# The opening of a transformer layer written as one list: squares in pairs on TensorE, low parts on VectorE, four tiles in the first batch

## The chip, the cores and the metric

The kernel runs on one core of a Trainium2 chip. The core has five engines, each with its own queue of instructions that it works off in order: TensorE (PE in the profile, with its weight loads as PEld), VectorE (DVE), ScalarE (ACT), GpSimd (POOL) and SyncE (SP), which here issues transfers. PSUM, into which TensorE adds up, is used here as eight banks of 128 x 512 numbers.

The metric is the device time of one execution in microseconds (us). The kernel before takes 1415.44 us, the median of 3 runs (1415.26 to 1416.74). The profile comes from one execution of its own, which took 1416.67 us.

## What is computed

One layer on 1024 positions of width 1024, in float32. Cut to what the change touches:

```
cond = silu(c)                                  # one row of 1024
mod  = cond @ w_ada + b_ada                     # six vectors of 1024: shift and scale here, others later
h    = rms_norm(x, g) * (1 + scale) + shift     # the opening
proj = h @ w_in                                 # k, v, 4 tiles of q, 8 of the mLSTM's q and k, its v, its gates, its output gate
...                                             # attention with rotary angles; a bidirectional mLSTM; output projection; FFN; final norm
```

The root mean square is taken over the width of `x`, for each position.

## The kernel before

**Layout.** `x` lies transposed: eight slices of 128 rows (width) by 1024 columns (positions), each handled as two halves of 512 columns. A sum over the width is thus a sum over the partitions of all slices, and a matmul with a matrix of ones makes it and spreads it over all partitions.

**Precision.** A product is made of three fast matmuls: each factor is split into a high part (a copy rounded to the matmul's format, made by ACT) and a low part (the rest, by a subtraction). `mm3` (L297) does high times high (L298), weight high times input low (L299), weight low times input high (L300). Weight tiles come as pieces of 128 x 512: loaded to `wst`, split to `whi` by ACT and to `wlo` by POOL (L436 to L447). `ones` and the sums of squares are plain float32, and such a matmul is recorded as two instructions.

**The opening (L490 to L610).** The condition row is broadcast to 128 partitions by its transfer and put through Silu. Sixteen half slices are squared by ACT and added up by DVE and POOL into `ssx`; after warming matmuls (L550) two matmuls (L552) finish the sum, and `rstd_steps` (L533) makes the reciprocal root: ACT's root, one step of refinement on DVE. In between, `w_ada` arrives in blocks of 128 x 1024: block `j` times the condition, summed along the row (`ada_load`, L509), gives 128 numbers of `mod`; slice `k` needs blocks `k` (shift) and `8+k` (scale). Block 0 is summed by POOL and ACT, the others by one DVE instruction. Then for each slice (`h_steps`, L561): DVE multiplies by the root, ACT applies scale and shift, ACT makes the high part `hh`, POOL the low part `hl` (DVE for slice 0).

**The first batch (L600 to L610).** Three tiles of 128 output columns, the keys, the values and the first query tile, are summed up side by side over the eight slices: 3 tiles x 2 halves x 8 slices x 3 = 144 matmuls, in six banks, with two more for the sums of squares. Behind it come units one after the other (the list `IN`, L48): the gates with half of the values (`("t", 0)`, matmuls 272 columns wide), three query tiles of 48 matmuls each, then mLSTM tiles. The finished keys go through `rope_steps` (L616): two copies out of PSUM by ACT, a swap of rows by transfers, multiplications with the angles on POOL and DVE, a root, and at the end two copies `k2` split by ACT and POOL. A query tile goes through the same steps, without the copies. Attention starts when the last query tile and the gates' chain are done.

**What sets the order.** A planner in the kernel's Python code (`Clock`, L125) runs as the program is written. It keeps its own time, with a cost for each operation of DVE, ACT and POOL (`Engine.cost`, L99) and for transfers; `ck.chain` starts each step at the time at which it believes the last one to be over, `ck.pe` moves its time on for matmuls, and a unit goes on when its inputs are due. What it writes is a fixed order for each engine; the waits are real. `dve`, `act` and `gps` are the engines as the planner counts them; `nc.vector` and the like are the engines uncounted. `psum_any` takes a bank without telling the planner that it is in use.

## Time and profile before

| | |
|---|---|
| median of 3 runs | 1415.44 us (1415.26 to 1416.74) |
| profiled execution | 1416.67 us, span 1414.9 us |
| mean granted TensorE clock | 0.970 |
| first projection matmul | at 35.93 us |
| first matmul of the gate unit, behind the first batch | at 88.64 us |
| idle of TensorE from 160 to 208 us | 9.2 us (48.0 less 38.83 busy) |

A line of the timeline gives the start and the duration in us, the engine, the line of the program, the operation, the tile written and the tiles read, the shapes, how many such instructions follow one another, and in square brackets how long the engine stood idle before and what ended that. `L96` is the line of a helper through which most operations of DVE, ACT and POOL pass, so these are told apart by their tiles. TensorE's matmuls overlap in part, so their durations say less than the distance from one start to the next.

### The profile page before, as it was taken

Reading aid. Unit: us, or ns where it says so; the run is one execution under the profiler, and the core shown is the slowest. Engines: PE = TensorE matmul, PEld = TensorE weight load, DVE = VectorE, ACT = ScalarE, POOL = GpSimd, SP = SyncE. Lnnn points to the kernel's source line nnn. Section 1 sums busy time; section 2 is a strip of 40 time slices with the busy share of each in tenths; the row PEclk is TensorE's granted clock in tenths of the full one; section 3 lists DMA queues with packets and bytes.
Section 4 is the critical chain, followed back from the end, with each engine's and each line's share of the span. In section 5 each row is a group of like instructions: output and inputs, shape, how many; then the busy total and the mean of one; then the engine's idle time right before and its main releaser. Section 6 shows DMA issues by size and latency. Waiting matters only on the chain.

```text
span 1414.9 us, 19493 instructions
## 1 busy us (share of the span) xinstructions
PE 1305.6 (92%) x6594; PEld 1076.0 (76%) x6602; DVE 1078.5 (76%) x1564; ACT 660.8 (47%) x1192; POOL 733.9 (52%) x591
## 2 busy tenths in 40 slices
PE   5789799999999989899987899999999999979997
PEld 2578677888878978777765788888888887867886
DVE  7947989987888938777699786676666654998876
ACT  6444326677666655454565233233333333444462
POOL 5555454544345336677658554545445445545542
PEclk9899989999999999999998999999999999989999
DMA  7446452322122146653641342323322259823324
GB/s 294 155 127 201 148 157 79 120 64 65 49 64 59 36 158 189 226 179 122 200 149 58 99 157 92 109 98 112 112 94 85 83 164 315 302 82 100 94 64 153
DMA packets 103171, 184.39 MB, mean 130 GB/s; under 512 B 11296, under 2 KB 32672, under 8 KB 103072
## 3 DMA queue, kind: packets, MB, share of 16 engines
q1 hardware_dynamic: 89968, 161.06, 35.9%
q10 hardware_dynamic: 13104, 22.10, 4.2%
q8 instruction: 52, 0.85, 0.3%
q14 instruction: 47, 0.39, 0.1%
HBM read 136.19 MB, written 43.25 MB: 127 GB/s over the span
## 4 chain that ended last, share of the span: by engine, by line
PE 60%; DVE 21%; DMA 6%; issue 5%; ACT 4%; POOL 4%; SPq 1%; ACTq 0%; DVEq 0%; POOLq 0%
PE acc L299 15%; PE acc L298 15%; PE acc L300 15%; DVE x L96 4%; DVE ada L96 3%; PE av L1028 3%; DVE sst L96 2%; PE T L1009 2%; DVE PT L96 2%; PE S L977 2%; DVE y L96 1%; PE acct L298 1%; PE acct L300 1%; PE acct L299 1%; DMA qd<-q_d 1%
## 5 line engine op out<-in xcount | busy, mean ns | idle before, releaser
L96 POOL TENSOR_TENSOR wlo<-wst,whi 128x512 fp32r<-128x512 f32 (+2 forms) x208 | 297.5, 1436 | 261.2 <-ACT whi L96 249.8
L96 ACT ACTIVATE whi<-wst 128x512 fp32r<-128x512 f32 (+2 forms) x219 | 131.5, 605 | 121.2 <-PE acc L300 26.5
L96 POOL TENSOR_SCALAR P<-P,sst 128x1024 f32<-128x1024 f32 x64 | 88.8, 1391 | 141.1 <-DVE sst L96 98.0
L299 PE MATMUL acc<-x,whi 128*128 128x512 f32 x352 | 139.9, 398 | 1.1 <-DVE x L96 1.1
L96 POOL TENSOR_TENSOR wlo<-wr,whi 128x512 fp32r<-128x512 f32 x60 | 82.9, 1382 | 80.6 <-ACT whi L96 79.3
L298 PE MATMUL acc<-hh,whi 128*128 128x512 f32 x224 | 97.5, 435 | 14.1 <-ACT hh L96 11.8
L298 PE MATMUL acc<-whi,wch 128*128 128x512 f32 x244 | 97.1, 398 | 5.7 <-ACT wch L96 5.7
L96 ACT ACTIVATE P<-S,sst,colq 128x1024 f32<-128x1024 f32 x64 | 77.2, 1206 | 52.4 <-DVE sst L96 46.8
L299 PE MATMUL acc<-hl,whi 128*128 128x512 f32 x224 | 92.4, 413 | 8.2 <-POOL hl L96 4.5
L300 PE MATMUL acc<-whi,wcl 128*128 128x512 f32 x244 | 97.0, 398 | 2.9 <-DVE wcl L96 2.8
L299 PE MATMUL acc<-wlo,wch 128*128 128x512 f32 x244 | 97.1, 398 | 0.1
L96 DVE SCALAR_TENSOR_TENSOR ada<-ada,cond 128x512 f32<-128x512 f32 (+1 forms) x79 | 81.2, 1036 | 17.6 <-DMA ada<-in_w_ada_dram 12.1
L300 PE MATMUL acc<-hh,wlo 128*128 128x512 f32 x224 | 91.5, 408 | 0.0
L96 DVE TENSOR_TENSOR sg<-acc,sg 128x512 f32<-128x512 f32 x67 | 45.3, 686 | 60.4 <-PE acc L300 60.0
L96 ACT ACTIVATE PT<-T 128x512 fp32r<-128x512 f32 x128 | 71.4, 597 | 37.6 <-PE T L1009 36.8
L96 ACT ACTIVATE whi<-wr 128x512 fp32r<-128x512 f32 x60 | 37.8, 632 | 109.1 <-DVE wr L96 51.1
L96 DVE TENSOR_TENSOR PT<-T,PT 128x512 fp32r<-128x512 f32 x128 | 82.7, 681 | 7.3 <-ACT PT L96 7.1
L298 PE MATMUL acct<-whi,hh 128*128 128x256 f32 (+1 forms) x256 | 79.4, 310 | 2.5 <-ACT xp L96 1.1
L96 DVE TENSOR_TENSOR wcl<-wd,wch 128x512 fp32r<-128x512 f32 x50 | 50.9, 1031 | 38.6 <-ACT wch L96 38.3
L1009 PE MATMUL T<-con,P 128*128 128x128 f32 x512 | 70.3, 275 | 10.3 <-DVE PT L96 7.4
L299 PEld LDWEIGHTS acc<-x,whi 128*128 128x128 f32 x352 | 66.9, 190 | 16.8 <-DVE x L96 1.6
L96 POOL TENSOR_TENSOR wlo<-s,whi 128x512 fp32r<-128x512 f32 x44 | 59.5, 1353 | 38.0 <-ACT whi L96 32.1
...
## 6 DMA issues: line engine op xcount, KB each, us to landing
...
```

The source lines that it names most:

```text
L96: return fn(*args, **kw)
L298: nc.tensor.matmul(acc, w[0], x[0], start=first, stop=False)
L299: nc.tensor.matmul(acc, w[0], x[1], start=False, stop=False)
L300: nc.tensor.matmul(acc, w[1], x[0], start=False, stop=last)
L977: nc.tensor.matmul(sp[:, halves(n)], qs[:, j * P:(j + 1) * P], k2[g][m][:, halves(n)], start=m == 0, stop=m == 1)
L1009: nc.tensor.transpose(tp[:, k], Pt[q][:, (4 * b + k) * P:(4 * b + k + 1) * P], ident)
L1028: nc.tensor.matmul(av, va[:, k, h // 4], PT[it][m][:, k], start=(k, m) == (0, 0), stop=(k, m) == (NJ - 1, 1))
```

## The change

The opening is no longer planned. It is written out as one list for each engine, on the engines uncounted:

- The condition arrives as one row (a tile of zeros with the row in its first partition), gets its Silu there, and is spread by matmuls with `ones`, from which ACT copies it to all partitions.
- Whole slices are squared. DVE adds each odd slice's squares to the even one's, and TensorE sums the four pairs in PSUM, 8 matmuls, with a warming matmul behind each of the first three pairs. The warming matmuls go from 9 and 6 to 3 and 5.
- Both factors, root and scale, go on in one DVE instruction (`xr`); ACT adds the shift as it makes the high part; DVE makes all low parts (`h_lo_of`). All dot products are on DVE. POOL keeps the low parts of the weights.
- The batch has four tiles, with the second query tile: 192 matmuls, all eight banks. Its weights are loaded at the start, some of them into tiles that are used for keys and values later. The second query tile leaves `IN`, and its rope steps wait for both key copies.
- The constants come later, and the copies of the masks stand behind the batch. The planner's time is set to 24 us at the start of the batch and goes on by 0.23 for each matmul.

The diff, cut to its core (removed lines of the old opening are those shown above):

```
-WARM = 6
-WARM0 = 9
-POOLED = (0,)
+WARM = 5
+WARM0 = 3
+NT0 = 4
 NB = 3
 KB = 5
 AHEAD = 2
 NP = NF // 2
-IN = ([("t", 0), ("q", 1), ("q", 2), ("q", 3), ("f", 0), ("f", 4), ("f", 1), ("f", 5), ("t", 2), ("f", 2), ("f", 6),
+IN = ([("t", 0), ("q", 2), ("q", 3), ("f", 0), ("f", 4), ("f", 1), ("f", 5), ("t", 2), ("f", 2), ("f", 6),
...
-    both = const.tile([P, 2], F32, name="both")
+    both = const.tile([P, 3], F32, name="both")
...
-    nc.scalar.dma_start(con, cons)
-    nc.vector.tensor_copy(selr, C("sel"))
...
+        cond0 = PP["cond"] = bp.tile([P, D], F32, name="cond", bufs=1)
-        va = kvp.tile([P, NJ, 2, P], F32R, name="va")
-        k2 = [[kvp.tile([P, S], F32R, name=f"k2{i}{g}") for i in range(2)] for g in range(2)]
...
-        specs = conv_w(0) + conv_w(1) + conv_w(2)
+        specs = []
...
-        load_cond(bp)
...
-                        (gps if n and k < 6 else dve).tensor_add(ssx[n], ssx[n], sq)
...
+        ve, ac, gp = nc.vector, nc.scalar, nc.gpsimd
...
+        spare = [kvp.tile([P, S], F32, tag=f"k2{i}", name="spare") for i in range(3)]
+        crow = kvp.tile([P, S], F32, tag="k23", name="crow")
+        room = [t[:, halves(i)].rearrange("p (a b) -> p a b", a=4) for t in spare for i in range(2)]
+        x_t = [stp.tile([P, S], F32, tag="x", name=f"x{k}", bufs=KT) for k in range(KT)]
+        gp.memset(crow, 0.0)
+        nc.sync.dma_start(crow[0:1], c)
+        for k in range(KT):
+            nc.sync.dma_start(x_t[k], xT[k])
+        ada_t, wst_t = {}, {}
+        def ada_load(j):
+            ada_t[j] = bp.tile([P, D], F32, tag="big", name="ada")
+            nc.sync.dma_start(ada_t[j], w_ada[j])
+        def first_load(b, f):
+            i = 4 * b + f
+            wst_t[b, f] = (wp.tile([P, 4, P], F32, tag="wst", name="wst", bufs=3) if i < 3 else room[i - 3])
+            nc.sync.dma_start(wst_t[b, f], w_f[f][:, 4 * b:4 * b + 4])
+        for j in (8, 0):
+            ada_load(j)
+        for f in range(NT0):
+            first_load(0, f)
+        for j in (9, 1, 10):
+            ada_load(j)
+        nc.sync.dma_start(con, cons)
+        for f in range(NT0):
+            first_load(1, f)
+        W0 = {}
+        def first_hi(b, f):
+            if (b, f) in ((1, 2), (1, 3)):
+                i = 2 * (f - 2)
+                if not i:
+                    W0["more"] = kvp.tile([P, 4, 4, P], F32R, tag="va", name="more")
+                W0[b, f] = [W0["more"][:, i + j] for j in range(2)]
+            else:
+                W0[b, f] = [wp.tile([P, 4, P], F32R, tag="w" + t, name="w" + t) for t in ("hi", "lo")]
+            ac.activation(W0[b, f][0], wst_t[b, f], AF.Copy)
+        def first_lo(b, f, eng):
+            eng.tensor_sub(W0[b, f][1], wst_t[b, f], W0[b, f][0].bitcast(F32))
+        def dot(j):
+            ve.scalar_tensor_tensor(ada_t[j], ada_t[j], 1.0, cond0, op0=OP.mult, op1=OP.mult, accum_out=modacc[:, 0, j:j + 1])
+        sc1 = stp.tile([P, KT], F32, name="sc1")
+        b1 = stp.tile([P, KT], F32, name="b1")
+        ve.tensor_scalar(b1, V("b_ada", 8, KT), 1.0, None, op0=OP.add)
+        def shift(k):
+            ve.tensor_add(mod[:, k:k + 1], modacc[:, 0, k:k + 1], V("b_ada", k))
+        def gain(k):
+            ve.scalar_tensor_tensor(sc1[:, k:k + 1], modacc[:, 0, 8 + k:9 + k], b1[:, k:k + 1], V("norm_mix_g", k),
+                                    op0=OP.add, op1=OP.mult)
+        cb = [psum_any([P, HALF], "acc") for _ in range(NH)]
+        ac.activation(both[:, 2:3], eps, AF.Silu)
+        ac.activation(crow[0:1], crow[0:1], AF.Silu)
+        ac.activation(both[:, 2:3], eps, AF.Abs_reciprocal_sqrt)
+        for n in range(NH):
+            nc.tensor.matmul(cb[n], ones, crow[:, halves(n)], start=True, stop=True)
+        msp = [psum_any([P, HALF], "ms") for _ in range(NH)]
+        acc0 = [[psum_any([P, HALF], "acc") for _ in range(NH)] for _ in range(2)]
         for _ in range(WARM0):
...
+            nc.tensor.matmul(acc0[0][0], ones, crow[:, 0:HALF], start=True, stop=True)
+        ssx = stp.tile([P, S], F32, tag="ssx", name="ssx")
+        sqw = kvp.tile([P, 2, S], F32, tag="va", name="sqw")
+        sqs = [ssx, sqw[:, 0], sqw[:, 1]]
+        for k in range(KT):
+            if k == 2:
+                for n in range(NH):
+                    ac.activation(cond0[:, halves(n)], cb[n], AF.Copy)
+            t = sqs[2] if k % 2 else sqs[k // 2 % 2]
+            for cs in [slice(0, S)] if k < KT - 1 else [halves(n) for n in range(NH)]:
+                ac.activation(t[:, cs], x_t[k][:, cs], AF.Square)
+                if k % 2:
+                    a = sqs[k // 2 % 2]
+                    ve.tensor_add(a[:, cs], a[:, cs], t[:, cs])
+            if k % 2:
+                for n in range(NH):
+                    nc.tensor.matmul(msp[n], ones, a[:, halves(n)], start=k == 1, stop=k == KT - 1)
+                if k < KT - 1:
+                    nc.tensor.matmul(acc0[0][0], ones, crow[:, 0:HALF], start=True, stop=True)
+        rv, ry = ([small() for _ in range(NH)] for _ in range(2))
+        rstd = ry
+        def root_v(n):
+            ve.tensor_scalar(rv[n], msp[n], 1.0 / D, EPS, op0=OP.mult, op1=OP.add)
+        def root_y(n):
+            ac.activation(ry[n], msp[n], AF.Abs_reciprocal_sqrt, scale=1.0 / D, bias=eps)
+        def root_end(n):
+            ve.scalar_tensor_tensor(rv[n], rv[n], -0.5, msp[n], op0=OP.mult, op1=OP.mult)
+            ve.scalar_tensor_tensor(ry[n], rv[n], 1.5, ry[n], op0=OP.add, op1=OP.mult)
         for _ in range(WARM):
...
+            nc.tensor.matmul(acc0[0][0], ones, crow[:, 0:HALF], start=True, stop=True)
+        def xr(k, n):
+            x = x_t[k][:, halves(n)]
+            ve.scalar_tensor_tensor(x, x, sc1[:, k:k + 1], rstd[n], op0=OP.mult, op1=OP.mult)
+        def h_hi_of(k, n):
+            ac.activation(h_hi[k][:, halves(n)], x_t[k][:, halves(n)], AF.Identity, bias=mod[:, k:k + 1])
+        def h_lo_of(k, n):
+            ve.scalar_tensor_tensor(h_lo[k][:, halves(n)], x_t[k][:, halves(n)], mod[:, k:k + 1],
+                                    h_hi[k][:, halves(n)].bitcast(F32), op0=OP.add, op1=OP.subtract)
+        dot(8)
+        gain(0)
+        root_v(0)
+        root_y(0)
+        ac.activation(msp[0], ry[0], AF.Square)
+        first_hi(0, 0)
+        first_lo(0, 0, gp)
+        dot(0)
+        shift(0)
+        root_y(1)
+        root_end(0)
+        first_hi(0, 1)
+        first_lo(0, 1, gp)
+        xr(0, 0)
+        h_hi_of(0, 0)
+        root_v(1)
+        ac.activation(msp[1], ry[1], AF.Square)
+        first_hi(0, 2)
+        first_lo(0, 2, gp)
+        h_lo_of(0, 0)
+        first_hi(0, 3)
+        first_lo(0, 3, gp)
+        root_end(1)
+        xr(0, 1)
+        h_hi_of(0, 1)
+        h_lo_of(0, 1)
+        def prepare(k):
+            if k + 1 < KT:
+                if k > 1:
+                    ada_load(9 + k)
+                ada_load(k + 1)
+            dot(8 + k)
+            gain(k)
+            dot(k)
+            shift(k)
             for n in range(NH):
...
+                xr(k, n)
+                h_hi_of(k, n)
+            for n in range(NH):
+                h_lo_of(k, n)
+            if k < 5:
+                first_hi(1, k - 1)
+                first_lo(1, k - 1, gp)
+        def mm(k, f, n, i):
+            w, h = W0[k // 4, f], (h_hi[k][:, halves(n)], h_lo[k][:, halves(n)])
+            a, b = ((0, 0), (0, 1), (1, 0))[i]
+            nc.tensor.matmul(acc0[f][n], w[a][:, k % 4], h[b], start=(k, i) == (0, 0), stop=(k, i) == (KT - 1, 2))
+        acc0 += [[psum_any([P, HALF], "acc") for _ in range(NH)] for _ in range(2)]
+        ck.until(24.0)
         for k in range(KT):
...
+            if k + 1 < KT:
+                prepare(k + 1)
+            seq = [(f, n, i) for n in range(NH) for f in range(NT0) for i in range(3)]
+            if k == 0:
+                seq = [(f, n, i) for n in range(NH) for i in range(3) for f in range(NT0)]
+            elif k == KT - 1:
+                seq = [(f, n, i) for f in range(NT0) for n in range(NH) for i in range(3)]
+            for f, n, i in seq:
+                mm(k, f, n, i)
+                ck.pe(0.23)
+                if n == 1 and i == 2 and (k == 3 or k == 7 and f < 2):
+                    load_piece()
+        va = kvp.tile([P, NJ, 2, P], F32R, tag="va", name="va")
+        k2 = [[kvp.tile([P, S], F32R, tag=f"k2{2 * g + i}", name=f"k2{i}{g}") for i in range(2)] for g in range(2)]
+        ve.tensor_copy(selr, C("sel"))
+        ve.tensor_copy(identb, ident)
+        for i in range(2):
+            ve.tensor_copy(maskb[:, 0, i], C("maskf"))
+            ve.tensor_copy(maskb[:, 1, i], C("maskb"))
         att = {}
...
         dexp = mid.tile([64, 2 * MH, NJ], F32, name="dexp")
         un = Stream(units(IN))
+        rope_steps(4, [(a, Flag()) for a in acc0[0]])
         v_steps([(a, Flag()) for a in acc0[1]])
-        rope_steps(4, [(a, Flag()) for a in acc0[0]])
         ck.at(2.5, lambda: rope_steps(0, [(a, Flag()) for a in acc0[2]]))
+        ck.chain(0.0, *k2_ok, lambda: rope_steps(1, [(a, Flag()) for a in acc0[3]]))
         for i in range(2):
             rp.append(stp.tile([P, S], F32, tag="x", name="rps", bufs=KT))
             dma(rp[i], rope[i])
```

89 lines of the change are left out of this document (removed).

## The prediction

> **What bounds the kernel now.** I read the page first, then the busy time of each engine in stretches of the opening and behind it, then the chain of waits and the opening instruction by instruction. The page shows TensorE (PE) busy 92% of the span, so a change that leaves its work alone can gain only where PE stands still.
>
> ```profile
> span 1414.9 us, 19493 instructions
> PE 1305.6 (92%) x6594; PEld 1076.0 (76%) x6602; DVE 1078.5 (76%) x1564; ACT 660.8 (47%) x1192; POOL 733.9 (52%) x591
> ```
>
> The stretches (columns: stretch, its length, busy time of PE, weight loads, VectorE (DVE), ScalarE (ACT), GpSimd (POOL), granted PE clock, DMA share, GB/s):
>
> ```profile
> 28.70:40.40 11.70, 0.80 (x1) 0.29 (x1) 11.63 (x19) 7.11 (x11) 6.30 (x5) 0.73 0.83 294
> 40.40:88.64 48.24, 39.02 (x144) 28.98 (x144) 35.70 (x52) 20.62 (x32) 27.20 (x18) 0.89 0.42 137
> 88.64:120.00 31.36, 31.36 (x239) 29.91 (x237) 21.59 (x38) 11.97 (x24) 12.90 (x7) 1.00 0.52 139
> 120.00:160.00 40.00, 36.70 (x160) 29.55 (x158) 35.38 (x42) 17.32 (x24) 25.70 (x15) 0.91 0.56 175
> 160.00:208.00 48.00, 38.83 (x161) 30.93 (x162) 38.81 (x61) 13.38 (x20) 24.23 (x17) 0.89 0.57 175
> 208.00:508.00 300.00, 283.95 (x1877) 249.39 (x1876) 252.90 (x431) 196.94 (x343) 131.14 (x98) 1.00 0.22 66
> ```
>
> In the opening PE waits and DVE works: DVE is busy 11.63 of 11.70 us just before the projection. From 40.40 to 88.64 PE runs 144 matmuls. How long these need unhindered is in the timeline of PE:
>
> ```profile
> 35.93 0.80 PE L298 MATMUL acc<-hh,whi 128*128 128x512 f32 x1 [7.24 <-ACT hh L96]
> 40.45 0.80 PE L299 MATMUL acc<-hl,whi 128*128 128x512 f32 x1 [3.73 <-DVE hl L96]
> 41.04 0.63 PE L300 MATMUL acc<-hh,wlo 128*128 128x512 f32 x1
> 41.47 0.63 PE L298 MATMUL acc<-hh,whi 128*128 128x512 f32 x1
> ...
> 56.95 0.50 PE L299 MATMUL acc<-hl,whi 128*128 128x512 f32 x1 [1.39 <-POOL hl L96]
> ...
> 77.72 0.79 PE L298 MATMUL acc<-hh,whi 128*128 128x512 f32 x1 [4.55 <-ACT hh L96]
> ...
> 83.02 0.40 PE L298 MATMUL acc<-hh,whi 128*128 128x512 f32 x1
> ...
> 88.64 0.29 PE L298 MATMUL acct<-whi,hh 128*128 128x272 f32 x1
> 88.77 0.29 PE L299 MATMUL acct<-wlo,hh 128*128 128x272 f32 x1
> ```
>
> The 24 matmuls from 83.02 to 88.64 take 5.62 us, 0.234 each; at the lower clock they are 0.43 apart (41.04 to 41.47). So 144 need 33.7 us of 48.2, and 14.5 us are waits and low clock. The chain of waits names DVE for them: the dot products (ada) and the scaling of the input (x) hold 37% of the chain up to 92 us.
>
> ```profile
> by line: DVE ada L96 22.1%; DVE x L96 15.2%; DVE mod L96 8.5%; DMA x<-in_xT_dram 7.6%; POOL ssx L96 6.6%; issue 4.6%; PE acc L299 3.9%; DVE hl L96 3.6%; PE acc L300 3.5%; DVE ssx L96 3.4%; PE acc L298 3.2%; ACT sq L96 2.7%; DVE sc L96 2.5%;
> ```
>
> **The gain on offer.** The change puts the first query tile's 48 matmuls into the opening batch. Before, that tile came behind the opening: 48 x 0.234 = 11.2 us. The old opening and that tile thus end, as PE time, at 88.64 + 11.2 = 99.8 us. The new batch, 192 x 0.234 = 44.9 us, has to be set against this.
>
> **Step 1, to the sum of squares.** The condition row now comes first, behind a memset of 0.95 us on POOL that the sync queue waits for; then Silu of one row. TensorE spreads the row to all partitions (2 full-precision matmuls), runs 3 for warmth, 8 for the squares with 3 between: 16, each recorded as two halves.
>
> ```profile
> 5.27 1.06 ACT L96 ACTIVATE cond<-cond 128x1024 f32<-128x1024 f32 x1 [2.34 <-DMA cond<-in_c_dram]
> 7.61 10.95 PE L550 MATMUL acc<-con,ones 128*128 128x512 f32 x18 [7.61 <-DMA con<-in_cons_dram]
> 12.86 0.34 PEld L550 LDWEIGHTS acc<-con,ones 128*128 128x128 f32 x1 [0.52 <-issue]
> 13.68 0.19 PEld L550 LDWEIGHTS acc<-con,ones 128*128 128x128 f32 x1 [0.48 <-issue]
> 14.11 0.19 PEld L550 LDWEIGHTS acc<-con,ones 128*128 128x128 f32 x1 [0.24 <-issue]
> 19.66 1.12 PE L552 MATMUL ms<-ssx,ones 128*128 128x512 f32 x2 [1.10 <-DVE ssx L96]
> 81.43 0.95 POOL L96 MEMSET gI<- 128x1024 f32 x1
> ```
>
> A half takes 0.43 us (13.68 to 14.11) once the clock is up and about 0.85 in the first 6.1 us (7.61 to 13.68; 7 halves). The old broadcast of half a megabyte had landed by 5.27; the row is 4 KB but issued 0.7 us later, so I take 4.1, and PE starts at 5.2. It is PE that sets this step: square 4 reuses the buffer that the first pair's matmuls read. 5.2 + 6.1 + 25 x 0.43 = 22.0 for the second half of the columns, 21.1 for the first; before it was 19.66 + 1.12 = 20.8. So the squares on TensorE gain nothing here, and freeing POOL of its additions gains nothing either. Bounds 20 to 22.5, from a row 1 us earlier or 1.2 us later.
>
> The Trainium skill, "TensorE: Matmul & The Clock Gate", section "Part 1: The HAM clock gate", has the clock up after about 3.4 us of work; the row above shows 6.1. By that rule, an estimate, the low-clock phase would be 2.7 us shorter, the step 1.3 us and the sum as much; I keep the row.
>
> **Step 2, to the first projection matmul.** Durations:
>
> ```profile
> 20.82 0.69 ACT L96 ACTIVATE sq<-ms,both 128x512 f32<-128x512 f32 x1 [1.01 <-PE ms L552]
> 24.68 0.59 ACT L96 ACTIVATE ms<-sq 128x512 f32<-128x512 f32 x1
> 31.69 0.61 ACT L96 ACTIVATE hh<-x 128x512 fp32r<-128x512 f32 x1
> 29.73 0.68 DVE L96 TENSOR_TENSOR x<-x,sq 128x512 f32<-128x512 f32 x1
> 30.33 1.22 DVE L96 SCALAR_TENSOR_TENSOR ada<-ada,cond 128x1024 f32<-128x1024 f32 x1
> 31.48 0.08 DVE L96 DVE_READ_ACCUMULATOR ada<-ada,cond 128x1 f32 x1
> 45.10 0.68 DVE L96 TENSOR_TENSOR x<-x,sq 128x512 f32<-128x512 f32 x1
> 47.38 1.30 POOL L96 TENSOR_TENSOR hl<-x,hh 128x512 fp32r<-128x512 f32 x1 [3.62 <-ACT hh L96]
> 49.48 2.31 DVE L96 SCALAR_TENSOR_TENSOR ada<-ada,cond 128x1024 f32<-128x1024 f32 x1
> 57.09 0.69 DVE L96 TENSOR_TENSOR x<-x,sq 128x512 f32<-128x512 f32 x1
> 73.95 2.35 DVE L96 TENSOR_TENSOR x<-x,sq 128x512 f32<-128x512 f32 x2
> ```
>
> A half row on DVE occupies 0.60 us (29.73 to 30.33), a dot product 1.15 (30.33 to 31.48). But a dot product beside a POOL operation takes 2.31: it stands until POOL is done. From 45.10 to 57.09 two of the eight 128-row slices pass: own work 4 x 0.6 + 4 x 1.15 + 0.5 small = 7.5 of 12.0 us, with four POOL operations, so each costs DVE 1.1 us. New order: root 0.69 (to 21.8), root_v and the second dot product on DVE to 23.2, two root steps and the scaling, 3 x 0.6, with two weight splits of POOL in between, 2 x 1.1 to 1.25: 26.9; high part on ACT, 0.61 to 0.81: first matmul at 27.7, against 35.93 before. Bounds 25.4 (POOL costs nothing) and 29 (one more operation, step 1 late).
>
> The Trainium skill, "SBUF — State Buffer", section "Who interferes with whom", has GpSimd and a VectorE operation with two SBUF inputs take turns on one port, held for the whole instruction: 1.30 per POOL operation instead of 1.1. By that, an estimate, the opening's ten operations below would end it 2 us later.
>
> **Step 3, the batch.** Slice 0 waits for its four weight tiles one by one (ACT 0.61, POOL 1.30 each): its last matmul is near 36. DVE goes on from 26.9 with one root_v, four half rows and a scaling (3.7), two POOL operations (2.2) and 1.1 of waiting for ACT, to 33.9; with slice 1's dot products, scaling and high part (2.5 + 0.6 + 0.6) its first matmul is ready at 37.5. From then on each slice needs on DVE two dot products 2.3, two small ones 0.2, two scalings and the two low parts 2.4, together 4.9, and about 0.4 of waiting for ACT's high part: 5.3. PE needs 5.6. Low parts moved from POOL add 1.2 us a slice to DVE, but POOL's 1.1 twice a slice go. What stays on POOL are weight splits: four of the second weight half, one per slice 1 to 4, then the next unit's, about three against slice 6 and one against 7. Starts of slices by DVE: 37.5, then 4 x (5.1 + 1.1) = 62.3 for slice 5, + 5.1 + 3.3 = 70.7, + 6.2 = 76.9 for slice 7. Behind it PE waits 0.7 for the low part, 0.5 for the second column half, and runs 5.4: **83.5**. So the fourth tile is covered by PE's waits, and the batch gains 99.8 - 83.5 = 16.3. Bounds: POOL free of cost, 35.5 + 0.7 + 7 x 5.6 = 75.4 (gain 24.4); each POOL operation 1.3 and step 2 at its late end, 88 (gain 11.8). ACT has 2 x 0.81 + 0.61 = 2.2 us a slice and hides. Weight and ada transfers hide too: POOL frees the staging tiles by 32, and an ada tile is asked for two slices (12 us) ahead.
>
> **Step 4, behind the opening.** Four tiles hold all eight PSUM banks. The pair of the fourth is read only when both key copies are ready:
>
> ```profile
> 119.18 5.21 POOL L96 TENSOR_TENSOR k<-kdup,k 128x1024 fp32r<-128x1024 f32 x2 [10.35 <-ACT k L96]
> 93.75 1.35 DVE L96 TENSOR_SCALAR sq<-ms 128x512 f32<-128x512 f32 x2 [17.44 <-ACT sq L96]
> 100.55 0.68 DVE L96 SCALAR_TENSOR_TENSOR sq<-sq,ms 128x512 f32<-128x512 f32 x1
> 8.12 0.22 DVE L295 CAST maskb<-con 128x128 bf16<-128x128 f32 x1
> ```
>
> Before, that was at 124.4, 36 us behind the batch. So the gate and value unit starts with six banks, while the key's root (2), the value's transposes (2) and the query's sums (1) want some, and DVE empties the unit's own late. Price: 0 if ACT, idle there, empties tiles 0 to 2 in time, 9 if PE stands behind the unit's first column block (88.64 + 24 x 0.13 = 91.8) until the root has read its banks (100.55); I take 2.5, nearer the first, since tiles 0 and 1 finish 18 and 12 matmuls, 4.2 and 2.8 us, before the batch does. The query's rope steps now load DVE and POOL beside the gates' chain: DVE is at 84% between 120 and 208 (35.38 + 38.81 of 88), so between 0 and 5; I take 1.5. The six small copies of masks move behind the opening: at most 6 x 0.22 us on DVE, idle there for 17.44 us, so nothing; without that cover 1.3.
>
> **Sum.** 16.3 - 2.5 - 1.5 = 12.3. The profiled run took 1416.67 us (span 1414.9 and 1.8 around it): 1404.4. It lies 1.2 above the median of 1415.44, so on the median's footing **1403**. Bounds of the parts together: gains of 24.4 and of -2.2 (11.8 - 9 - 5).
>
> **Rivals.** (A) DVE, not PE, sets the pace behind the opening as well. For: 84% there, and its idle 17.44 us before 93.75 is all that shrinks. Then the moved matmuls return as PE idle, and only the earlier end counts: 88.6 - 83.5 = 5.1, 1410. Against: from 208 to 508 PE is busy 284 of 300, DVE 253. (B) POOL costs DVE nothing, because its splits fall into DVE's waits: gain 24.4 - 2.5, about 1394. Against: 2.31 for 1.22. (C) Slower: the new pauses hold PE's clock down. A matmul at the low clock costs 0.43 - 0.234 = 0.196 more; from 78 such of 192 on (15.1 us) the change is over 0.2% slower, and with 120 (23.5) it is 11.2 slower, 1427. For: after pauses of 3.7 and 4.55 us the next ones are 0.43 apart. Against: after 1.39 us (56.95) they were not, and my longest pause is about 2.2. (D) The change lands but the order that the planner writes behind it does not close up: PE idle from 120 to 208, 3.3 + 9.2 = 12.5 us, doubles, and 12.3 are gone: 1415.5, no change.
>
> **How the numbers follow.** Forecast 0.56, A 0.20, B 0.08, C 0.06, D 0.10. About 0.2%, 2.8 us, is what a measurement of this kernel can tell from no change. Faster: forecast, B and most of A (0.18), 0.82. Same: 0.06 of D and 0.02 of A, 0.08. Slower: C and the 0.04 of D in which more than the gain goes, 0.10. The range leaves out C and the worst of D above, and half of B below: 1393 to 1414.
>
> **What would show it.** Sums of squares no earlier than 20 us; first projection matmul near 28; the batch's 192 matmuls ending between 80 and 87 with DVE above 90% busy; dot products near 2.3 beside a weight split and 1.22 elsewhere; waits of PE in the gate unit for ACT or DVE under 5 us together; attention's first scores 8 to 20 us earlier than before. The prediction is wrong in its core if the batch ends after 92, if its matmuls are 0.43 apart for more than 15 us, or if the batch ends as said and the scores start no earlier.

## The result, and the profile after

The changed kernel takes 1433.82 us (median of 4 runs, 1433.20 to 1434.39); the kernel before has a median of 1416.09 (4 runs). The recorded ratio is 1.0106, with a 95% interval of 1.0087 to 1.0124. The ratio stands for 15 us and the medians are 17.7 us apart, so the change is slower by 15 to 18 us; forecast was a gain of 12. The profiled run took 1433.2 us.

The opening itself came out nearly as predicted. From TensorE's timeline of the changed kernel (start, duration, then what ended the idle time before):

```profile
4.39 3.78 PE L564 MATMUL acc<-crow,ones 128*128 128x512 f32 x4 [4.39 <-ACT crow L561]
...
19.02 1.88 PE L586 MATMUL ms<-sqw,ones 128*128 128x512 f32 x4
...
27.05 0.73 PE L667 MATMUL acc<-hh,whi 128*128 128x512 f32 x2 [1.86 <-ACT hh L611]
...
72.97 0.50 PE L667 MATMUL acc<-hh,whi 128*128 128x512 f32 x1 [2.39 <-ACT hh L611]
...
86.05 0.39 PE L667 MATMUL acc<-hh,more 128*128 128x512 f32 x1
86.28 0.29 PE L292 MATMUL acct<-whi,hh 128*128 128x272 f32 x1
```

The first projection matmul is at 27.05 (before 35.93), and all four tiles are summed up at 86.28, where the three tiles took until 88.64. Counting the fourth tile's 11.2 us, the opening is 99.8 - 86.28 = 13.5 us better. Between 27.05 and 86.28 VectorE is the busier engine, with 52.58 of 59.23 us (TensorE 50.35), and from the second to the seventh slice it sets the pace, with 6.7 us or more a slice (see step 3 below):

```profile
27.05:86.28 59.23, 50.35 (x192) 36.68 (x193) 52.58 (x81) 20.35 (x35) 19.23 (x13) 0.97 0.44 148
```

So the loss is behind the opening. I cut both runs at three events that both have, the first scores of attention, its last value matmul (`av`) and the first sum of squares of the second norm, and read busy time by stretch (stretch, length, PE, weight loads, DVE, ACT, POOL, granted PE clock, DMA share, GB/s). Before:

```profile
0.00:205.10 205.10, 162.17 (x721) 124.61 (x722) 159.03 (x234) 88.41 (x137) 108.01 (x70) 0.92 0.56 182
205.10:504.80 299.70, 284.58 (x1872) 249.68 (x1870) 254.90 (x428) 196.56 (x342) 133.95 (x101) 1.00 0.23 67
504.80:695.20 190.40, 174.85 (x992) 148.22 (x998) 131.68 (x285) 95.02 (x235) 125.03 (x159) 0.97 0.58 186
```

After:

```profile
0.00:198.70 198.70, 169.12 (x750) 128.31 (x751) 155.70 (x230) 76.18 (x117) 84.19 (x53) 0.95 0.55 180
198.70:511.00 312.30, 296.18 (x1971) 262.85 (x1969) 257.13 (x438) 198.56 (x350) 132.88 (x101) 0.99 0.25 74
511.00:710.60 199.60, 165.78 (x871) 137.23 (x877) 129.22 (x285) 89.68 (x225) 120.80 (x154) 0.91 0.53 170
```

The lengths differ by -6.4, +12.6 and +9.2 us; what comes behind the third event takes 719.7 us before (1414.9 - 695.2) and 720.8 after (1431.4 - 710.6). Together that is the whole difference of the spans, 16.5 us, and each of the first three parts can be read further.

**Ahead of attention, -6.4 instead of -13.5.** The last rows of the gate columns come to VectorE behind an adaLN dot product whose load is late (timeline of VectorE after):

```profile
117.61 2.11 DVE L96 SCALAR_TENSOR_TENSOR ada<-ada,cond 128x512 f32<-128x512 f32 x1 [5.19 <-DMA ada<-in_w_ada_dram]
...
119.65 0.16 DVE L96 COPY gI<-acct 128x16 f32<-128x16 f32 x1
```

The gates' chain starts from that copy, at 119.65. In the kernel before, the last of the eight copies was at 117.3 (count, shortest/median/longest ns, first to last start):

```profile
L96 DVE COPY gI<-acct x8: 159/163/175, 96.2 to 117.3; 128x16 f32<-128x16 f32 x8
```

**In attention, +12.6.** TensorE stood still 16.1 us (312.30 - 296.18), before 15.1. TensorE did 11.6 us more in the longer stage, with 432 column matmuls of the value and output-gate units (`acct`, 3 x 144), before 312 (3 x 104). These are fill work: units that the planner puts wherever attention leaves TensorE free. That the stage is longer because of them is how I first read this; the experiments do not bear it out (e1 and e17 below). One of the three forms, before and after:

```profile
L298 PE MATMUL acct<-whi,hh 128*128 128x256 f32 x104 | 32.4, 312 | 1.5 <-ACT xp L96 1.1 <-ACT vstg L96 0.5
```

```profile
L292 PE MATMUL acct<-whi,hh 128*128 128x256 f32 x144 | 43.5, 302 | 0.0
```

**Behind attention, +9.2.** There TensorE had 9.1 us less to do and stood still for 33.8 us (199.60 - 165.78), before 15.6 (190.40 - 174.85). Groups of TensorE's instructions in that stretch, before and then after (count, busy time and mean, then idle time in front and what ended it):

```profile
L298 PE MATMUL acct<-whi,hh 128*128 128x256 f32 x88 | 28.0, 318 | 0.9 <-DVE avt L96 0.9
L1795 PE MATMUL ni<-Cs,mq 128*128 128x260 f32 x64 | 21.0, 411 | 6.8 <-DVE num L96 6.7
```

```profile
L292 PE MATMUL acct<-whi,hh 128*128 128x256 f32 x48 | 14.4, 300 | 0.9 <-DVE avt L96 0.9
L1875 PE MATMUL ni<-Cs,mq 128*128 128x260 f32 x64 | 21.6, 421 | 19.0 <-DVE num L96 19.0
```

Of the column matmuls 3 x 48 = 144 were left there, before 3 x 88 = 264, and the mLSTM's own matmuls waited 19.0 us for VectorE's `num` instead of 6.7. One place stands out. The column units ended at 537.3 us, the first output unit (`yah`) began at 558.1; before, 581.9 and 582.5. All matmuls of the two kinds, before and then after:

```profile
L300 PE MATMUL acct<-whi,hl x256: 274/282/293, 88.9 to 581.9; 128*128 128x256 f32 x96, 128*128 128x272 f32 x32
L298 PE MATMUL acc<-yah,whi x128: 389/397/793, 582.5 to 715.1; 128*128 128x512 f32 x128
```

```profile
L294 PE MATMUL acct<-whi,hl x256: 274/283/292, 86.5 to 537.3; 128*128 128x256 f32 x96, 128*128 128x272 f32 x32
L292 PE MATMUL acc<-yah,whi x128: 391/397/994, 558.1 to 730.5; 128*128 128x512 f32 x128
```

The timelines of TensorE and of VectorE at the end of that gap:

```profile
556.39 1.21 PE L1875 MATMUL ni<-Cs,mq 128*128 128x260 f32 x2 [8.58 <-DVE num L96]
```

```profile
554.72 0.69 DVE L96 SCALAR_TENSOR_TENSOR ada<-ada,cond 128x512 f32<-128x512 f32 x1 [0.78 <-DMA ada<-in_w_ada_dram]
...
555.63 0.61 DVE L96 SCALAR_TENSOR_TENSOR num<-ni,cols,num 128x130 f32<-128x130 f32 x2
```

No output unit may start before the last 16 half loads of `w_ada` are in, for the memory they use is given to the output units. When the column units run out, the kernel's loop (`while not summed`) takes the remaining loads one after the other, and the `num` that TensorE waits for stands behind them on VectorE. A second stop comes near the end of the stretch: TensorE waits 4.55 us for ScalarE's `yah`, up to 678.96, and 2.87 us for GpSimd's `yal`, up to 682.63. By then these loads have long been in.

### The profile page after: what moved, and what is told of

Read it like the earlier page. It is cut to its first block, busy times and chain, and to the rows that moved or that the text cites. A ratio compares the mean times of both kernels' runs of the same rounds, so it can differ in the third digit from the quotient of the medians.

```text
span 1431.4 us, 19460 instructions
## 1 busy us (share of the span) xinstructions
PE 1314.7 (92%) x6602; PEld 1081.2 (76%) x6610; DVE 1074.5 (75%) x1569; ACT 645.8 (45%) x1171; POOL 706.5 (49%) x572
## 4 chain that ended last, share of the span: by engine, by line
PE 56%; DVE 25%; issue 6%; POOL 4%; DMA 4%; ACT 4%; SPq 0%; DVEq 0%; ACTq 0%; POOLq 0%
PE acc L293 14%; PE acc L294 14%; PE acc L292 14%; DVE sst L96 4%; DVE y L96 3%; DVE x L96 3%; PE av L1108 3%; DVE PT L96 2%; PE S L1057 2%; PE T L1089 2%; DVE ada L96 1%; DVE ada L545 1%; POOL wlo L96 1%; DVE qg L96 1%; POOL wv L96 1%
## 5 line engine op out<-in xcount | busy, mean ns | idle before, releaser
L96 POOL TENSOR_TENSOR wlo<-wst,whi 128x512 fp32r<-128x512 f32 (+2 forms) x200 | 288.2, 1447 | 267.2 <-ACT whi L96 257.1
L96 ACT ACTIVATE whi<-wst 128x512 fp32r<-128x512 f32 (+2 forms) x211 | 126.2, 605 | 118.9 <-PE acc L294 26.6
L96 POOL TENSOR_TENSOR wlo<-wr,whi 128x512 fp32r<-128x512 f32 x60 | 83.5, 1392 | 79.7 <-ACT whi L96 77.0
L96 DVE TENSOR_TENSOR PT<-T,PT 128x512 fp32r<-128x512 f32 x128 | 83.7, 682 | 12.7 <-ACT PT L96 12.5
L96 DVE TENSOR_REDUCE sst<-S 128x1 f32<-128x1024 f32 x64 | 77.7, 1214 | 4.8 <-PE S L1057 4.8
L96 DVE SCALAR_TENSOR_TENSOR x<-acc,mod,x 128x512 f32<-128x512 f32 (+1 forms) x92 | 62.6, 717 | 17.3 <-PE acc L294 17.1
L1108 PE MATMUL av<-PT,va 128*128 128x256 f32 x512 | 70.4, 283 | 4.0 <-DVE PT L96 4.0
L292 PE MATMUL acc<-hh,whi 128*128 128x512 f32 x160 | 70.3, 440 | 3.0 <-ACT xp L96 3.0
```

The lines of the kernel that those rows point to most:

```text
L96: return fn(*args, **kw)
L292: nc.tensor.matmul(acc, w[0], x[0], start=first, stop=False)
L1108: nc.tensor.matmul(av, va[:, k, h // 4], PT[it][m][:, k], start=(k, m) == (0, 0), stop=(k, m) == (NJ - 1, 1))
```

## The experiments

From the result I had two theories. *Lost cover*, or *stock*: the 48 matmuls moved into the first batch were fill work; the units behind them move up, and the stock is too small where the mLSTM's own chains set the time. *Order*, or *draw*: the planner writes a new order for any change ahead of it, and the kernel before happens to have a good one. A third, *gap*, came up on the way: the loop over the loads.

**e1_hold.** Lost cover taken back: the column units stop during attention with 264 matmuls left, as before (eleven chunks of 24; the "33" in the text below is a slip).

```
+ held = Flag()
...
- yield [pieces[w0 + k // 2][2]] + (...)
+ yield [pieces[w0 + k // 2][2]] + (...) + ([held] if (ci, j, k) == (1, 5, 0) else [])
...
  ck.streams([Stream(values()), Stream(turned()), Stream(scores())], [un])
+ held.set(ck, ck.t)
```

> The changed kernel, but its last 33 column chunks of the fill units t1 and t3 (264 matmuls of 256 columns, the number that the kernel before had left) are held back until the attention stage is over; nothing else is changed. Theory 'lost cover': the mLSTM stage is bound by its own chains and the attention stage by TensorE, so 120 matmuls x 0.122 us = 14.6 us go back to where they cost nothing. TensorE's idle time from the last av matmul to the first ms of norm2 falls from 33.8 us to near the 15.5 of the kernel before, attention ends about 12 us earlier, and the time is 1433 - 18 = 1415 us (1408 to 1421). Rival 'order': the planner's order, its clock set 18 us too early at the end of the first batch, puts waits in later stages whatever the stock of fill work is; the time stays within 4 us of 1433.

1426.74 us, ratio 1.0062 (1.0044 to 1.0080). Its stretches (attention, a piece of it, behind attention):

```profile
198.80:513.60 314.80, 289.51 (x1850) 253.72 (x1849) 256.85 (x438) 195.33 (x341) 127.94 (x97) 0.97 0.23 68
469.00:499.00 30.00, 22.37 (x124) 19.50 (x124) 19.32 (x35) 15.93 (x28) 6.71 (x6) 0.83 0.03 7
513.60:704.70 191.10, 175.10 (x991) 148.30 (x998) 132.35 (x285) 94.65 (x235) 126.40 (x158) 0.97 0.57 187
```

Behind attention the idle time fell from 33.8 to 16.0, as the theory said. But attention did not get shorter: without fill work, from 469 to 499, TensorE was busy 22.37 of 30 us. Attention at its end goes at a pace of its own; I had taken it for bound by TensorE. With the 312 column matmuls that the kernel before has there, it takes 314.8 us and not 299.7, so their number is not what makes the stage 12.6 us longer. Half of the theory held.

**e2_ada64.** The last 16 half loads go with attention: `ada_late(64)` for `ada_late()` in `scores`, with `mod_sum` defined earlier.

> The changed kernel, but the last 16 half loads of the adaLN weights with their dot products run in the attention stage, so the row of nine waits on VectorE between 518 and 555 us falls away. Theory 'lost cover': of the 18 us of idle TensorE time that came up behind attention, only the part that stands at these loads goes, the 8.6 us at 556; the units behind come earlier and run out earlier, so some of it comes back at 666 to 686: 1424 to 1432 us. Rival 'serial loads': this loop is the cause of the slower mLSTM stage, and all of its 11 us go: 1419 to 1423 us. If VectorE or the queues are short in the attention stage, it gets slower: above 1434 us.

1421.03 us, 1.0025 (1.0007 to 1.0043). The gap is 1.0 us, the idle time behind attention 24.2 with only 132 column matmuls left; the stretch takes 184.5 us, attention 317.1. The loop mattered here, as the rival said.

**e3_three.** The new opening, with three tiles in the batch.

```
-NT0 = 4
+NT0 = 3
...
-IN = ([("t", 0), ("q", 2), ...
+IN = ([("t", 0), ("q", 1), ("q", 2), ...
...
-        ck.chain(0.0, *k2_ok, lambda: rope_steps(1, [(a, Flag()) for a in acc0[3]]))
```

> The changed kernel with three tiles in its first batch; the fourth (query tile 1) is again the second fill unit, as in the kernel before. All the rest of the new opening stays. Theory 'lost cover': the stock of fill work is that of the kernel before, the batch is set by VectorE (6.7 us a slice, less a weight split) and ends near 80 us, 9 us earlier than before's 88.6, and the gates' chain with it; 1416 - 9 = 1407 us (1400 to 1414). Rival 'order': the waits of the later stages come from the planner's clock and the places of loads in the queues, which this kernel shares with the changed one: 1420 to 1435 us.

1411.84 us, 0.9959 (0.9944 to 0.9974): faster than before, and inside the range of the stock theory. But not for its reason alone. Scores start at 199.3, 5.8 us earlier; attention takes 307.5 (+7.8), the stretch behind it 189.8 (-0.6), with 192 column matmuls left and 20.1 us idle; and the rest takes 712.9 us, 6.8 less than before. So the rest alone is more than the 5.4 us by which the span is shorter. Only the kernels with three tiles (712.9 to 714.8) have that; in all others the rest takes 717.2 to 721.6. Why, I did not find.

**e4_noq1.** Fill work taken out of the kernel before, its opening untouched:

```
- mm3(acc, weights(w0, k, 4), ...)
- ck.pe(0.65)
+ w = weights(w0, k, 4)
+ if not (w0 == start["q", 1] and 0 < k < KT - 1):
+     mm3(acc, w, ...)
+     ck.pe(0.65)
```

> The kernel before, its opening untouched, with 36 of the 48 matmuls of the fill unit of query tile 1 left out (the six middle slices of the sum; the tile's values are then only part of the sum, everything else is computed). It takes 36 x 0.217 = 7.8 us of TensorE work out of the stock of fill work ahead of attention, as the changed kernel does by moving the tile into the first batch. Theory 'lost cover': the gates' chain and not TensorE bounds the stretch ahead of attention, so the later units move up and the cover is missing behind attention: no gain or a loss, 1414 to 1430 us. Rival 'TensorE bounds it': the time falls by the work that is gone: 1406 to 1410 us.

1446.89 us, 1.0202 (1.0176 to 1.0228). With 7.8 us of TensorE work less, the kernel is 29 us slower. That TensorE bounds the stretch ahead of attention is out; the first scores came 2.5 us earlier, at 202.6. The direction is that of lost cover, 177 column matmuls left and 34.2 us idle, but the size is beyond its range.

**e5_shift05, e6_shift2.** The kernel before with its planner's clock put ahead: `ck.until(ck.t + 0.5)`, or `+ 2.0`, behind the first batch. No work moves.

> The kernel before with one change that moves no work at all: behind the first batch the planner's clock is put 0.5 us ahead. The planner then writes another order from the batch on (the same fill units, the same instructions, TensorE's queue in another interleaving). Theory 'order': the kernel before is a favourable draw; each change ahead of the planner draws again, and a new draw costs mostly in the attention stage (300 us before, 308 to 317 in the four kernels run so far) and behind it. This kernel then takes 1420 to 1440 us, with an attention stage of 305 to 318 us. Rival 'stock': the order as such costs nothing, what counts is how much fill work is left at which stage, and that is the same here: 1412 to 1420 us, attention 298 to 303 us.

> As the run with 0.5 us, the planner's clock put 2 us ahead behind the first batch of the kernel before: a second draw of the order. Theory 'order': 1420 to 1440 us, attention 305 to 318 us. Rival 'stock': 1412 to 1420 us, attention 298 to 303 us.

1443.80 us, 1.0189 (1.0174 to 1.0204), and 1421.05 us, 1.0025 (1.0010 to 1.0041). Half a microsecond in the planner's model costs more than the whole change did. Attention and what follows, with 0.5:

```profile
204.80:517.70 312.90, 296.65 (x1953) 262.56 (x1952) 258.30 (x432) 197.66 (x348) 129.64 (x102) 0.98 0.24 70
517.70:723.70 206.00, 170.67 (x908) 142.22 (x913) 131.68 (x285) 91.98 (x229) 120.44 (x157) 0.91 0.52 166
```

These rows look like those of the changed kernel: 12 us more work in attention, a gap of 17.0 us, 35.3 us idle behind it. So this pattern needs no new opening; 180 column matmuls were left. With 2.0, 192 were left and 21.3 us idle. That the same fill list leaves the same stock at that point, as the rival assumed, is wrong; how much of it attention takes is itself part of the order.

**e7_no_ada.** In the changed kernel no late adaLN load is started before the gates' steps are written: `if started and ck.t > t_ada[0]` in `ready`, with `started` filled behind `gate_steps()`.

> The changed kernel, but in the stretch ahead of attention no adaLN half load is started before the gates' steps are written, so that none of their dot products stands on VectorE in front of the last copies of the gate columns (5.2 us of idle time at 117.6 in the changed kernel). The last copy comes at 113 to 115 us instead of 119.6, and the first scores 3 to 6 us earlier, at 193 to 196. Theory 'order': the time does not follow, since everything behind is written in a new order: anywhere from 1415 to 1440 us, by its attention stage. Rival 'gates': what the gates gain comes out at the end, 1427 to 1430 us.

1417.35 us, 1.0000 (0.9988 to 1.0012). All copies of the gate columns, and the scores:

```profile
L96 DVE COPY gI<-acct x8: 159/172/175, 89.4 to 114.8; 128x16 f32<-128x16 f32 x8
L1057 PE MATMUL S<-k,qs x256: 387/395/797, 189.8 to 487.3; 128*128 128x512 f32 x128
```

The last copy is at 114.8 and the first scores at 189.8, 15.3 us ahead of the kernel before and more than I expected: the place of those loads had cost the new opening the larger part of its gain. Behind it attention took 310.7 us; 240 column matmuls were left, 24.3 us idle.

**e8_three_ada64.** e3 and e2 together.

> The three-tile kernel (1411.8 us) with the last 16 half loads of the adaLN weights in the attention stage. In the changed kernel that move took 12 us off (1433 to 1421), with the stretch behind attention falling from 199 to 184 us and attention growing by 5 us. Theory 'serial loads': the same here, the stretch behind attention falls from 190 to 182 to 186 us; 1402 to 1410 us. Theory 'order': the gain of the first case is a draw, and this one is another: 1405 to 1430 us, with no tie to the loads.

1413.97 us, 0.9977 (0.9963 to 0.9992). The stretch behind attention fell from 189.8 to 187.0, not to the 182 to 186 expected, and attention took 1.2 us more: no gain over e3. With 192 left there was little for the loads to hold up.

**e9_after_ahead4, e10_shift05_ahead4, e11_before_ahead4.** Behind attention the loads are made four at a time: `ada_late(64, 4)` in the tick and in the loop; in the changed kernel, in e5 and in the kernel before.

> The changed kernel; only behind attention, the last 16 half loads of the adaLN weights are kept four at a time in flight instead of two. Theory 'gap': in the changed kernel the fill units ran out at 537 us while the loads were still being made two at a time, and no output unit may start before the last of them: 20.8 us from the last column chunk to the first output matmul (0.6 us in the kernel before), and TensorE idle for 33.8 us behind attention (15.6 before). Here the loads are done when the units run out, the 20.8 us become at most 5, the idle time 16 to 24 us, attention stays at 312 us, and the time is 1433 less 10 to 18: 1415 to 1423 us. Rival 'order': the stretch is one more draw and the gap is not what it hangs on; 1425 to 1440 us, or a gain with the gap still there.

> The kernel before with its planner's clock 0.5 us ahead (1443.8 us, a gap of 17.0 us, TensorE idle for 35.3 us behind attention), and the loads behind attention four at a time. Theory 'gap': the gap falls to at most 5 us, the idle time to 16 to 24, the time to 1425 to 1434 us; its attention stage, in which 11 us more fill work was done than in the kernel before, stays at 313 us. Rival 'order': 1436 to 1450 us.

> The kernel before with the loads behind attention four at a time. Its units last until 582 us, so there is no gap to close. Theory 'gap': no gain beyond the spread of a new order in that stretch, 1411 to 1420 us. Rival: the four loads are of use by themselves (earlier output units, less waiting of VectorE), 1403 to 1409 us.

1428.40 us (1.0074; 1.0051 to 1.0096), 1431.37 us (1.0099; 1.0073 to 1.0125) and 1434.67 us (1.0122; 1.0097 to 1.0147). For the changed kernel:

```profile
L294 PE MATMUL acct<-whi,hl x256: 274/282/292, 87.2 to 535.6; 128*128 128x256 f32 x96, 128*128 128x272 f32 x32
L292 PE MATMUL acc<-yah,whi x128: 389/397/796, 538.7 to 726.3; 128*128 128x512 f32 x128
```

```profile
511.10:706.40 195.30, 164.63 (x879) 135.03 (x878) 127.74 (x285) 90.22 (x225) 118.99 (x154) 0.94 0.52 174
```

The gap went from 20.8 to 3.1 us, and the idle time only from 33.8 to 30.7: TensorE waits elsewhere, 13.1 us in front of `ni` and 7.0 in front of `yah`. In e10 the gap fell from 17.0 to 4.9 and the idle time from 35.3 to 25.5. The kernel before got 18 us slower without any gap, which neither theory allows; its idle time rose to 27.2. That gives the gap a part in the loss of e5, and less in that of the changed kernel; it is not the whole cause of either.

**e12_three_late_ahead4.** e3, e7 and four loads at a time together.

> Three tiles in the first batch, no adaLN half load started before the gates' steps, and the loads behind attention four at a time. If the three causes add up: first scores near 187 us (189.8 with four tiles, less the 0 to 5 us by which the gates' columns came earlier with three), attention 308 to 312, a stretch behind it of 186 to 191, a rest of 713 to 720: 1397 to 1410 us. If each new order takes back what the opening gives, 1412 to 1425 us.

1410.30 us, 0.9947 (0.9928 to 0.9966), the lowest median of all, though not clear of e3: scores at 194.0, attention 309.4, behind it 187.4, the rest 714.8. It lies just outside the range where the causes add up; the scores come 7 us later than I added up.

**e13 to e16.** Two more draws for both kernels, by a constant of the planner's model: `PEL = 0.25` for 0.2, and `LAT = 0.15` for 0.14.

> The kernel before with one constant of the planner's model (the delay that it adds before a fill unit counts as ready) at 0.25 instead of 0.20 us. No instruction is added or left out; TensorE's queue is interleaved in another way. Theory 'draw': anywhere from 1418 to 1445 us, since the kernel before is a favourable draw (1416, against 1421 and 1444 in the two others). Rival 'change': 1413 to 1420 us.

> The changed kernel with the same constant at 0.25. Theory 'draw': anywhere from 1410 to 1440 us, as often below the kernel before with the same constant as above it. Rival 'change': 10 to 20 us above the kernel before with the same constant.

> The kernel before with another constant of the planner's model (the delay from one engine's end to the next one's start) at 0.15 instead of 0.14 us. Theory 'draw': 1418 to 1445 us. Rival 'change': 1413 to 1420 us.

> The changed kernel with that constant at 0.15. Theory 'draw': anywhere from 1410 to 1440 us, no tie to the same constant in the kernel before. Rival 'change': 10 to 20 us above the kernel before with the same constant.

The kernel before: 1416.28 us (0.9989; 0.9970 to 1.0008) and 1428.05 us (1.0070; 1.0048 to 1.0092). The changed kernel: 1434.25 us (1.0125; 1.0081 to 1.0170) and 1438.65 us (1.0151; 1.0117 to 1.0185). Of the two draws of the kernel before, the first lies in the range of 'change' and the second in that of 'draw'. By pairs the changed kernel is 17.7, 18.0 and 10.6 us slower. That speaks against the draw alone, though three pairs are few: the kernel before scatters from 1416 to 1444 in five draws, the changed kernel from 1434 to 1439 in three, and the two scatters overlap.

The draws also settle what the +12.6 us in attention are worth as evidence. In the four redraws of the kernel before, which move no work, attention takes 312.9, 306.5, 305.4 and 314.6 us, against 299.7; of all other kernels only e11 is near that, with 301.8, and it has the same order up to there. The 12.6 us of the changed kernel lie within what a new order alone makes.

TensorE's idle time behind attention goes with the stock in most of these kernels. Column matmuls left at attention's last `av`, TensorE's idle time from there to the second norm, and the distance from the last column matmul to the first output matmul, worked out as above:

| kernel | left | idle, us | gap, us | attention, us | time, us |
|---|---|---|---|---|---|
| e16, after, LAT | 132 | 43.7 | 1.1 | 315.9 | 1438.65 |
| e2, after, loads in attention | 132 | 24.2 | 1.0 | 317.1 | 1421.03 |
| after | 144 | 33.8 | 20.8 | 312.3 | 1433.82 |
| e14, after, PEL | 144 | 34.4 | 2.5 | 317.5 | 1434.25 |
| e9, after, four loads | 144 | 30.7 | 3.1 | 313.4 | 1428.40 |
| e4, before less fill | 177 | 34.2 | 17.1 | 315.5 | 1446.89 |
| e5, before, 0.5 | 180 | 35.3 | 17.0 | 312.9 | 1443.80 |
| e10, e5 with four loads | 180 | 25.5 | 4.9 | 313.1 | 1431.37 |
| e3, three tiles | 192 | 20.1 | 4.9 | 307.5 | 1411.84 |
| e12, three, late, four loads | 192 | 20.9 | 0.1 | 309.4 | 1410.30 |
| e6, before, 2.0 | 192 | 21.3 | 10.8 | 306.5 | 1421.05 |
| e13, before, PEL | 204 | 19.3 | 2.8 | 305.4 | 1416.28 |
| e15, before, LAT | 204 | 20.3 | 0.9 | 314.6 | 1428.05 |
| e8, three, loads in attention | 216 | 18.2 | 1.0 | 308.7 | 1413.97 |
| e7, after, late loads | 240 | 24.3 | 0.9 | 310.7 | 1417.35 |
| before | 264 | 15.6 | 0.6 | 299.7 | 1416.09 |
| e1, after, 264 held | 264 | 16.0 | 0.6 | 314.8 | 1426.74 |
| e11, before, four loads | 264 | 27.2 | 0.1 | 301.8 | 1434.67 |

Up to 180 left, 34 to 44 us idle where the loads behind attention are as in the kernel before, and 24 to 31 where they are moved or made four at a time; from 192 left, 16 to 24, but for e11. The time of the whole kernel does not follow the stock: e1 and e11 have 264 left and are slow. The gap does not sort the idle times: e14 and e16 have hardly any.

**e17_hold8, e18_lat_hold8.** The table is a correlation, so the last two runs set the count on purpose: the last column unit waits for the end of attention, `[held] if (ci, j, k) == (3, 0, 0)`, in the changed kernel and in e16.

> The changed kernel, with the last column unit (t3, 192 matmuls) held back until attention is over, so that 192 are left there instead of 144. Theory 'stock': attention gives up 48 x 0.122 = 5.9 us of TensorE work and may idle 1 to 3 us more; behind it the idle time falls from 33.8 to 19 to 22 us, with 5.9 us more work, so the stretch takes 189 to 194 us instead of 199.6; in all 1433 - 11 = 1422 us (1417 to 1426). Rival 'draw': the idle time is not set by this count; 1428 to 1440 us.

> The changed kernel with the planner's delay at 0.15 (1438.7 us, 132 column matmuls left, 43.7 us idle behind attention), and the last column unit held back in the same way. Theory 'stock': attention gives up 60 x 0.122 = 7.3 us of work, the idle time behind it falls to 19 to 22 us, the stretch from 204.9 to 187 to 192 us; in all 1439 - 19 = 1420 us (1415 to 1426). Rival 'draw': 1430 to 1445 us.

1414.92 us, 0.9978 (0.9960 to 0.9997), and 1426.74 us, 1.0056 (1.0037 to 1.0075): 18.9 and 11.9 us less than the kernels that they were made from (those were run at another time: against the kernel before beside each, 17.7 us more became 3.2 less, and 20.5 more became 8.6 more). For the first, attention, the stretch behind it, and the 30 us in which the changed kernel had its gap, followed by that row of the changed kernel:

```profile
198.90:511.30 312.40, 292.94 (x1922) 258.23 (x1921) 256.94 (x438) 198.09 (x348) 133.23 (x101) 0.99 0.24 73
511.30:694.20 182.90, 164.84 (x919) 137.59 (x925) 133.12 (x285) 91.13 (x228) 119.48 (x155) 0.99 0.57 187
530.00:560.00 30.00, 25.34 (x177) 23.29 (x178) 25.85 (x65) 16.32 (x47) 16.58 (x25) 1.00 0.69 221
```

```profile
530.00:560.00 30.00, 15.17 (x78) 12.58 (x79) 18.59 (x48) 7.54 (x23) 14.26 (x22) 0.69 0.68 225
```

Attention ends within 0.3 us of where it did, and the stretch behind it is 16.7 us shorter, with 18.1 us idle instead of 33.8. Holding back 48 matmuls of 0.122 us, 5.9 us of work, gave 16.7 us. The wait in front of `ni` fell from 19.0 us to 9.9:

```profile
L1877 PE MATMUL ni<-Cs,mq 128*128 128x260 f32 x64 | 20.5, 402 | 9.9 <-DVE num L96 9.6
```

The gap also fell, from 20.8 to 2.4 us, but it is not what the gain hangs on: in e16 and e18 it is 1.1 and 3.0, and the idle time fell there as well, from 43.7 to 24.9. The wait that went was another one, that of the mLSTM's `U`. The row of e16, then e18's row and its stretch behind attention:

```profile
L1791 PE MATMUL U<-wv,kt 128*128 128x260 f32 x64 | 18.1, 402 | 21.2 <-DVE Cs L96 21.2
```

```profile
L1793 PE MATMUL U<-wv,kt 128*128 128x260 f32 x64 | 16.6, 382 | 0.0
514.10:707.30 193.20, 168.28 (x920) 140.51 (x926) 128.50 (x285) 92.30 (x227) 117.17 (x154) 0.96 0.55 177
```

The gain is beyond my range (1417 to 1426) in the first kernel and just short of it (1415 to 1426) in the second, where 24.9 us idle remain and attention idles 23.3 instead of 18.1 us. Both lie under the ranges of the 'draw' rival (1428 to 1440, and 1430 to 1445). Holding a unit back also writes a new order behind attention, so the sizes carry that scatter; that two kernels, at two counts, both fall is what I rely on.

## Why the prediction was wrong

**Step 1** was 1 us off on the safe side: the sums of squares ended at 20.90 (19.02 + 1.88) instead of 22.0. TensorE started on the row of the condition at 4.39 instead of 5.2, and TensorE's clock was up after 5.0 us instead of 6.1. These rows of the weight loads are 0.85 us apart up to 8.82 and 0.43 from 9.39 on:

```profile
7.97 0.34 PEld L568 LDWEIGHTS acc<-crow,ones 128*128 128x128 f32 x1 [0.52 <-issue]
8.82 0.33 PEld L568 LDWEIGHTS acc<-crow,ones 128*128 128x128 f32 x1 [0.52 <-issue]
9.39 0.19 PEld L568 LDWEIGHTS acc<-crow,ones 128*128 128x128 f32 x1 [0.24 <-issue]
9.82 0.19 PEld L568 LDWEIGHTS acc<-crow,ones 128*128 128x128 f32 x1 [0.24 <-issue]
```

The 3.4 us of the Trainium skill ("TensorE: Matmul & The Clock Gate", "Part 1: The HAM clock gate") are shorter than the 5.0 here and the 6.1 before. The same section says that the window runs freely, so that a start may fall anywhere in it; two starts with two lengths agree with that.

**Step 2** was right, in part by luck: 27.05 for 27.7. Its terms as listed come to 27.2 for the end of the scaling (23.2 + 1.8 + 2.2), not 26.9, and step 1 gave 1 us back.

**Step 3** was right in kind and 2.8 us short: 86.28 for 83.5. A slice takes VectorE 6.7 us (38.70 to 45.40 and on to 58.82, the starts of each slice's first dot product), where I had 5.1 + 1.1 = 6.2; four slices make 2.0 us of the 2.8. The term that was too small is the slice's own work. I had worked out 5.3 for it and then added up 5.1; with 5.3 the sum comes to 84.7. Slice 6 met three weight splits of GpSimd at once, as forecast, and took 8.8 us (65.52 to 74.28) for 5.1 + 3.3 = 8.4:

```profile
38.70 2.32 DVE L545 SCALAR_TENSOR_TENSOR ada<-ada,cond 128x1024 f32<-128x1024 f32 x1
41.20 1.22 DVE L545 SCALAR_TENSOR_TENSOR ada<-ada,cond 128x1024 f32<-128x1024 f32 x1
61.18 0.22 DVE L555 SCALAR_TENSOR_TENSOR sc<-modacc,b,vec 128x1 f32<-128x1 f32 x1
67.95 1.20 DVE L555 SCALAR_TENSOR_TENSOR sc<-modacc,b,vec 128x1 f32<-128x1 f32 x1
```

```profile
65.45 6.03 POOL L96 TENSOR_TENSOR wlo<-wst,whi 128x544 fp32r<-128x544 f32 x3 [5.39 <-ACT whi L96]
```

The dot products behaved as forecast, 2.32 beside a split and 1.22 without. What I had not counted is that a small operation of 0.22 us stands as long, 1.20, and that the splits themselves stretch to 6.03 / 3 = 2.0 us. The Trainium skill ("SBUF — State Buffer", "Who interferes with whom") has the two engines hold the shared port for a whole instruction in turn; these rows agree in kind. The estimate by that rule, an end 2 us later, came near the 2.8 by luck: a dot product beside a split took 1.10 us more (2.32 - 1.22), the price that I had. VectorE was busy 52.58 / 59.23 = 89% where I had said above 90%.

**Step 4** looked at banks and at VectorE's load behind the opening, with 2.5 + 1.5 us. What stood there was neither: a late adaLN load in front of the gate columns. The first scores came 6.4 us earlier, not 8 to 20; e7, without those loads, has them 15.3 us earlier. The place was right, the resource wrong: I had not asked which instructions of later stages stand in VectorE's queue between the opening and the gate columns, and what these wait for.

**The sum** is the step that failed, and with it the part called "the gain on offer". It counted the moved tile as 48 x 0.234 = 11.2 us gained, and carried 12.3 us from the end of the batch to the end of the kernel. But a query tile behind the batch was fill work. Leaving such work out of the kernel before gained nothing: it became 29 us slower (e4, one draw). What the batch took in was missing at the other end of the list: 144 column matmuls behind attention instead of 264, 120 x 0.122 = 14.6 us, where 18.2 us of idle time took their place; and with 48 of them given back there, in e17, the kernel came to 1414.92. How much of the shortage comes from the moved tile and how much from the new order is open: e5 had 180 left with no tile moved. The sum had a second hole: it took attention's length as fixed, and attention came out 12.6 us longer, in e17 too (312.4). So with the stock at 192 the kernel is about level with the one before, not 12 us faster. I had read the page as if one bound held from the batch to the end, and the profile's row from 208 to 508 only as proof that TensorE is the busier engine. The stretch from 505 to 695, with its 15.6 us idle, I did not read at all, though each unit of the list that I shortened ends there.

**The rivals.** A (VectorE sets the pace behind the opening) had its price near what the scores showed, 5.1 against 6.4, for another reason. B did not occur. C did not either: one pause, 2.39 us at 72.97, was followed by eight matmuls 0.43 apart, 8 x 0.2 = 1.6 us. D is the nearest, the order behind does not close up; but its sign, that TensorE's idle time up to the first scores doubles, did not show (from 120 us on 12.6 us, before 12.5), for the loss came 300 us later, and it was not bounded by the gain.

**What is settled and what is not.** Shown: the new opening gains 13.5 us up to the end of the batch; 7 us of it are lost ahead of attention, and come back with the adaLN loads out of the way (e7); setting the column units' stock at 192 takes 12 to 19 us off the changed kernel, at two counts. Shown too: shifts that move no work changed the kernel before by -2, 3, 10 and 26 us against the runs beside them, so one pair of kernels cannot tell how much of the 15 to 18 us is the draw; that it has a part in it I infer from attention's length. Open: how large that part is; what in the order makes attention 300 us long in the kernel before and e11, and 305 to 318 in all others; why the idle time falls between 180 and 192 left (192 is one whole unit, but that is all I can say); why e11 is slow with its full stock; and where the three-tile kernels get their 7 us in the last 700.
